# The first 512 columns behind each inner norm in plain float32, in a two-layer transformer encoder

## The chip, the cores and the metric

The kernel runs on one core of a Trainium2 chip. The metric is the time of one execution in microseconds (us), taken on the device; the median of three executions before the change is 2357.82 us (2348.81 to 2362.06).

The names of the engines are those of the profile: PE multiplies matrices (PEld is its loading of weights), DVE is the vector engine, ACT the scalar engine, POOL the third one, SP issues the transfers (DMA) from main memory.

## What is computed

Two layers of an encoder over 256 tokens of width 2048, all in float32. In each layer a modulation vector `mod = silu(c) @ w_mod + b_mod` gives a shift, a scale and a gate for each of two halves. The two halves are the mixers and the FFN:

```python
h = layer_norm(x) * (1.0 + scale_m) + shift_m
proj = h @ w_in[l]
uv, q_c, kv_c, k_r, sb, sc, sh, ag = jnp.split(proj, IN_SPLITS, axis=-1)
...
y = jnp.concatenate([y_a, y_b, y_c, y_d], axis=-1) @ w_out[l]
x = layer_norm(ALPHA * x + (1.0 + gate_m) * y, post_mix_g[l], post_mix_b[l])
h = layer_norm(x) * (1.0 + scale_f) + shift_f
gate, val = jnp.split(h @ w_up, 2, axis=-1)
gate = causal_dwconv(gate, w_conv, b_conv)
y = (jax.nn.silu(gate) * val) @ w_down
x = layer_norm(ALPHA * x + (1.0 + gate_f) * y, post_ffn_g[l], post_ffn_b[l])
```

`y_a` is a gated MLP mixer (its two inputs are called U and V here), `y_b` an attention (B), `y_c` a short convolution (C and E), `y_d` a convolution of 31 taps with a norm over channels (D). The FFN is 5632 wide.

## The kernel before, in words

**Tiles.** The 256 tokens are two token tiles of 128. A product has the contraction of 2048 in 16 tiles of 128 (`kt`). The weights come from memory as `wraw`, 128 x 2048 floats each, on SP's queue. Outputs lie channel-major (128 channels on the partitions, 256 tokens beside one another) for the mixers and the FFN's first product, token-major for `w_out` and `w_down` (out_proj).

**Split products.** Most products are not done in plain float32. A weight tile is split into a rounded part `whi` (ACT, line 403) and the remainder `wlo` (DVE, line 404), an activation in the same way (`hT`, lines 422 and 423), and PE adds three products: `whi` with the high part of `hT`, `whi` with its low part, `wlo` with the high part. There are 4 buffers for `whi` and 4 for `wlo`. For the first items behind a norm a split may go to spare buffers instead (`thi`, `tlo`: the argument `spare`). Layer 0's mixers and a part of its w_out take unsplit float32 products with `wexact` tiles that need no ACT or DVE work; a `wexact` tile sits in a `whi` or `wlo` buffer.

**Groups.** `group` runs a block of columns over all 16 `kt` with moving operands of 256 tokens; `group2` does so with 512 (high and low part beside one another), and adds the two halves afterwards (ACT `second`, line 1200). `run` and `stream` put an item's loads, splits and products in program order, with the products of an item always one item behind its loads (`pending`, `flush`).

**The order on an engine.** Each engine runs its instructions in the order that a scheduler gave them from the program order and their dependences. What is told to wait behind a norm (`hold`: the next 4 splits and 6 modulation steps) is told so by a dependence.

**Inner norms.** There are three between the first product and the last: behind layer 0's w_out (called site 1 here), behind layer 0's w_down (site 2), behind layer 1's w_out (site 3). Out_proj ends with a residual, a LayerNorm `p` with gains, and the statistics of the next norm, `r` (DVE, lines 586 to 616, token tile 0 first, while PE multiplies token tile 1). Then `to_hT` does, for each token tile and each quarter (4 `kt`): `xn` on ACT (normalise), four transposes on PE (`ps_xT`, line 535), scale and shift on ACT (token tile 0) or DVE (token tile 1) into `hf`, and the split of `hf` into `hT`. The order of the eight steps interleaves the token tiles, and the first product takes all 256 tokens of a `kt`.

**Behind the norms.** Site 1 is followed by the FFN of layer 0: group `g0a` (1024 gate columns), interleaved by hand with `v0a` (512 value columns); its last quarter of `hT` is made in between (`LATE_KT`, a part of the modulation comes only then). Site 2 is followed by layer 1's mixers in the order D, U, V, B, C, E; site 3 by layer 1's FFN, beginning with a `group2`.

**Modulation.** The modulation's own weights pass through SP's queue in steps called mods here, each a DMA and a DVE step (line 211, 2.35 us for 128 x 2048), placed by a rate for each stage (`RATES`), at one or two of an item's loads. What a norm needs and what isn't there yet is done ahead of it at once (`need`, `needs`). PE sums the result over partitions (`ps_mod`). Small steps such as the convolution of D are spread by `bg` (`STEPS`), and what is left of them is drained at the end.

Of the kernel before, what the change touches and what calls it, by code (L numbers as in the profile page):

```python
# [13 lines left out]
P = 128  # L14
D = 2048
S = 256
DEPTH = 2
# [37 lines left out]
def encoder_kernel(ctx: ExitStack, tc: tile.TileContext, A: dict, consts: bass.AP, out: bass.AP):  # L55
# [262 lines left out]
    def phase(l, name):  # L318
        pace["rate"] = RATES[l][name]
# [97 lines left out]
    def new_hT():  # L417
        hT[:] = [act_pair("hT") for _ in range(KT // 2)]

    def split(dst, src):  # L420
        hi, lo = dst[:2]
# [103 lines left out]
    def to_hT(t, k0, nkt, r, l, m_shift, m_scale, hF=None):  # L525

        n = nkt * P
        xn = tmp_tile("xn")[:, :n]
        i = ident_act(xn, X[t][:, k0 * P : k0 * P + n], r[:, 0:1], r[:, 1:2])
        for m in (m_shift, m_scale):  # L530
            for name in {MOD_BY[(l, m, k0 + j)] for j in range(nkt)}:
                tc.add_manual_dep(i.ins, name, data_dep, reason="PSUM is free for the modulation first")
        ps = ms_tile("ps_xT")
        for j in range(nkt):
            pe.transpose(ps[:, j * P : (j + 1) * P], xn[:, j * P : (j + 1) * P], ident)  # L535
        if hF is None:
            h3 = tmp_tile("hf")[:, :n].rearrange("p (j t) -> p j t", j=nkt)
        else:
            h3 = hF[k0 // 4][:, k0 % 4 : k0 % 4 + nkt, t * P : (t + 1) * P]
        for j in range(nkt):  # L540
            src, dst = ps[:, j * P : (j + 1) * P], h3[:, j, :]
            sc, sh = MOD[(l, m_scale, k0 + j)], MOD[(l, m_shift, k0 + j)]
            if t == 0:
                ident_act(dst, src, sc, sh)
            else:
                dve.tensor_scalar(out=dst, in0=src, scalar1=sc, scalar2=sh, op0=ALU.mult, op1=ALU.add)  # L546
        for j in range(0, nkt, 2):
            hl = [h[:, :, t * P : (t + 1) * P] for h in hT[(k0 + j) // 2][:2]]
            split(hl, h3[:, j : j + 2, :])


    CHUNKS = ((0, 1024), (1024, 512), (1536, 512))

# [127 lines left out]
    def mixers(l, w_in, Y, hF=None, between=None):  # L681
# [467 lines left out]
    def ffn_up(l, G):  # L1149
        pf = PF[l]  # L1150
        w = A["ffn_w_up"][l]
        col = lambda k, j: pf[:, k * NF + j : k * NF + j + 1]
        def gated_pairs(cps, _):
            for b in range(4):
                if b % 2 == 0:
                    G.append(slot("g").rearrange("p (j s) -> p j s", j=4))
                src = cps[b].rearrange("p (j s) -> p j s", j=2)
                act.copy(G[b // 2][:, 2 * (b % 2) : 2 * (b % 2) + 2, :], src)
            for j in range(8):
                background.append(lambda j=j: gate_conv(j))  # L1160

        def valued_pairs(cps, _):
            drain_background()
            for b in range(2):
# [3 lines left out]
        def gate_conv(j):  # L1168
# [6 lines left out]
                )  # L1175
            act.activation(out=x, in_=u, func=AF.Silu)

        if l == 0:
# [8 lines left out]
            for g, u in ((gg, 5), (gv, 2), (gg, 6), (gg, 7), (gv, 3)):  # L1187
                stream(lambda: g[1](u), lambda item, g=g, u=u: g[2](item, u))
            pending.extend([gg[3], gv[3]])

        for c0 in range(0, D_FF, 512):
            gi, j0 = c0 // 512, c0 // P
# [90 lines left out]

        return before

    after_norm = []

    def modulated(l, m_shift, m_scale, quarters=4):
        def rest(r):
            needs(l, m_shift, m_scale)()  # L1290
            for q in range(quarters, 4):
                for t in range(2):
                    to_hT(t, 4 * q, 4, r[t], l, m_shift, m_scale)

        def then(r):
            if quarters < 4:
                after_norm.append(lambda: rest(r))
            new_hT()
            for kind, n in (("split", 4), ("mod", 6)):
                hold[kind] = [last_norm[0].ins.name, n]  # L1300
            for t, q in ((0, 0), (0, 1), (1, 0), (0, 2), (1, 1), (0, 3), (1, 2), (1, 3)):
                if q < quarters:
                    to_hT(t, 4 * q, 4, r[t], l, m_shift, m_scale)

        return then

    def gate(l, m):
        def make():
# [5 lines left out]
    for l in range(DEPTH):  # L1314
        Y = {}
        if l == 0:
            hF = [slot(f"hF{q}").rearrange("p (j s) -> p j s", j=4) for q in range(4)]
            mixers(l, A["w_in"][l], Y, hF, lambda q: piece(q, hF))
        else:
            mixers(l, A["w_in"][l], Y)  # L1320
        phase(l, "out")
        flush()
        out_proj(
            l,
            A["w_out"][l],
            [Y[n] for n in "abcd"],
            list(range(KT)),
            gate(l, GATE_M),
            f"o{l}",
            A["post_mix_g"][l],  # L1330
            A["post_mix_b"][l],
            needs(l, SHIFT_F, SCALE_F, k1=LATE_KT if l == 0 else KT),
            modulated(l, SHIFT_F, SCALE_F, LATE_KT // 4 if l == 0 else 4),
            plain=(1024, 1536) if l == 0 else (),
        )
# [7 lines left out]
        out_proj(  # L1343
            l,
            A["ffn_w_down"][l],
            G,
            list(range(NF)),
            gate(l, GATE_F),
            f"d{l}",
            A["post_ffn_g"][l],  # L1350
            A["post_ffn_b"][l],
            needs(l + 1, SHIFT_M, SCALE_M) if l + 1 < DEPTH else None,
            modulated(l + 1, SHIFT_M, SCALE_M) if l + 1 < DEPTH else None,
        )
    flush()

# [62 lines left out]
```

## Time and profile before

| | us |
|---|---|
| median of three executions | 2357.82 (2348.81 to 2362.06) |
| span of the profiled execution | 2350.0 |
| PE busy in it | 2259.1 |
| DVE busy | 1811.3 |
| ACT busy | 1036.4 |
| PE waiting for `xn` ahead of the transposes at L535 (10 waits) | 36.5 |

Only the span is recorded of the profiled execution, not a time of its own; it lies inside the range of the three executions, 7.8 us under their median. In the profile's lines a group is named line, engine, operation, output<-inputs; sizes are partitions x elements. A float32 product shows as two records, a split (fp32r) one as one record. A timeline's row has the start, the time to the end of the run of equal instructions, and in brackets the idle time ahead of it with what ended it.

### The profile page before, as it was taken

How to read it: one execution, taken by the hardware profiler on the slowest of the kernel's cores; microseconds unless marked ns; L12 is line 12 of the kernel's file. 1: busy time of each engine (PE TensorE's matmuls, PEld its weight loads, DVE VectorE, ACT ScalarE, POOL GpSimd, SP SyncE). 2: the span in 40 equal slices, each digit the busy share in tenths (PEclk: the TensorE clock that was granted, in tenths of full speed). 3: DMA queues.
4: the chain of work that ended last, by engine and by line, in shares of the span. 5: the costliest groups of instructions: out<-in, count | busy, mean ns of one | idle time of the engine just before them, and what ended most of it. 6: DMA issues, size and time to landing. Idle time of an engine off the chain costs nothing. (4 is left out here: it accounts for less than half of the span.)

```text
span 2350.0 us, 30996 instructions
## 1 busy us (share of the span) xinstructions
PE 2259.1 (96%) x12183; PEld 1924.6 (82%) x12183; DVE 1811.3 (77%) x2293; ACT 1036.4 (44%) x1478; POOL 38.0 (2%) x59
## 2 busy tenths in 40 slices
PE   6899999799999999999989999989999999999998
PEld 4688886498888888888878999867888888888786
DVE  6868987789888887988976986787676656665676
ACT  2221241345455544544535434435454455554553
POOL 2000000000000000000000000000000000000000
PEclk9899999899999999999998999999999999999999
DMA  9999779498889898898756566856767655556554
GB/s 338 368 316 329 285 274 383 159 341 309 308 312 329 291 327 296 309 328 294 274 186 228 191 227 199 297 185 233 236 234 247 205 190 181 193 183 197 179 197 144
DMA packets 226491, 605.17 MB, mean 258 GB/s; under 512 B 14484, under 2 KB 27012, under 8 KB 208676
## 3 DMA queue, kind: packets, MB, share of 16 engines
q1 hardware_dynamic: 225560, 602.29, 73.2%
q8 instruction: 95, 1.56, 0.3%
q0 software_dynamic: 784, 0.90, 0.1%
q14 instruction: 52, 0.43, 0.0%
HBM read 601.05 MB, written 2.10 MB: 257 GB/s over the span
## 5 line engine op out<-in xcount | busy, mean ns | idle before, releaser
L404 DVE TENSOR_TENSOR wlo<-wraw,whi 128x1024 fp32r<-128x1024 f32 (+1 forms) x645 | 775.7, 1216 | 360.4 <-ACT whi L403 354.5
L403 ACT CAST whi<-wraw 128x1024 fp32r<-128x1024 f32 (+1 forms) x645 | 670.9, 1046 | 817.8 <-PE g_c L83 208.2
L83 PE MATMUL v_c<-hT,whi 128*128 128x512 f32 x1344 | 473.1, 397 | 0.0
L83 PE MATMUL g_c<-hT,whi 128*128 128x512 f32 x1272 | 450.3, 398 | 0.0
L83 PE MATMUL d<-whi,a 128*128 128x512 f32 x1344 | 388.4, 391 | 0.3 <-ACT whi L403 0.3
L211 DVE SCALAR_TENSOR_TENSOR macc<-wmod,cact,macc 128x2048 f32<-128x2048 f32 (+2 forms) x180 | 358.1, 1993 | 38.9 <-DMA wmod<-in_w_mod_dram 38.2
L83 PE MATMUL v_c<-hT,wlo 128*128 128x256 f32 x1344 | 376.9, 281 | 0.0
L83 PE MATMUL g_c<-hT,wlo 128*128 128x256 f32 x1272 | 358.2, 282 | 0.0
L83 PEld LDWEIGHTS v_c<-hT,whi 128*128 128x128 f32 x1344 | 252.3, 188 | 60.1
L83 PEld LDWEIGHTS d<-whi,a 128*128 128x128 f32 x1344 | 252.9, 188 | 53.7 <-ACT whi L403 0.8
L83 PEld LDWEIGHTS g_c<-hT,whi 128*128 128x128 f32 x1272 | 239.7, 188 | 57.4 <-issue 0.5
L83 PEld LDWEIGHTS v_c<-hT,wlo 128*128 128x128 f32 x1344 | 254.0, 189 | 0.3 <-DVE wlo L404 0.2
L83 PEld LDWEIGHTS g_c<-hT,wlo 128*128 128x128 f32 x1272 | 241.4, 190 | 0.7 <-issue 0.5
L83 PE MATMUL d<-wlo,a 128*128 128x512 f32 x672 | 234.4, 391 | 0.8 <-DVE wlo L404 0.8
L83 PEld LDWEIGHTS d<-wlo,a 128*128 128x128 f32 x672 | 126.6, 188 | 27.6 <-DVE wlo L404 1.1
L83 PE MATMUL o<-whi,a 128*128 128x512 f32 x352 | 99.6, 392 | 0.1
L708 DVE SCALAR_TENSOR_TENSOR convD<-gluD,pm,convD 128x245 f32<-128x245 f32 (+23 forms) x240 | 98.7, 467 | 0.5
L423 DVE TENSOR_TENSOR a<-g,a 128x512 fp32r<-128x512 f32 x132 | 89.0, 686 | 0.0
L83 PE MATMUL D_c<-hT,whi 128*128 128x256 f32 x432 | 83.9, 294 | 2.5 <-ACT hT L422 2.0
L422 ACT CAST a<-g 128x512 fp32r<-128x512 f32 x132 | 81.3, 616 | 7.2 <-PE d L83 6.0
L211 DVE SCALAR_TENSOR_TENSOR qacc<-wmod,cact,qacc 128x1024 f32<-128x1024 f32 (+1 forms) x75 | 80.3, 1070 | 2.6 <-DMA wmod<-in_w_mod_dram 0.5
L83 PEld LDWEIGHTS o<-whi,a 128*128 128x128 f32 x352 | 66.0, 188 | 14.4 <-ACT whi L403 0.5
(310 smaller groups left out, 2667.4 us busy)
## 6 DMA issues: line engine op xcount, KB each, us to landing
wraw<-in_ffn_w_up_dram SPq DMA_DIRECT2D x176, 1024.0 KB, 5.4
wmod<-in_w_mod_dram SPq DMA_DIRECT2D x136, 1024.0 KB, 5.7
wraw<-in_ffn_w_down_dram SPq DMA_DIRECT2D x88, 1024.0 KB, 5.2
wraw<-in_w_in_dram SPq DMA_DIRECT2D x34, 1024.0 KB, 5.9
wmod<-in_w_mod_dram SPq DMA_DIRECT2D x64, 512.0 KB, 8.0
wmod<-in_w_mod_dram SPq DMA_DIRECT2D x32, 768.0 KB, 6.8
wraw<-in_w_out_dram SPq DMA_DIRECT2D x24, 1024.0 KB, 7.3
wexact<-in_w_in_dram SPq DMA_DIRECT2D x44, 512.0 KB, 6.5
```

Of the source, the lines that this page charges most:

```text
L83: pe.matmul(o, lhsT, rhs, start=start, stop=stop, skip_group_check=True)
L211: i = dve.scalar_tensor_tensor(out=acc, in0=w, scalar=col, in1=acc, op0=ALU.mult, op1=ALU.add)
L403: act.copy(hi[:, :m], r)
L404: i = dve.tensor_tensor(out=lo[:, :m], in0=r, in1=hi[:, :m].bitcast(F32), op=ALU.subtract)
L422: act.copy(hi, src)
L423: dve.tensor_tensor(out=lo, in0=src, in1=hi.bitcast(F32), op=ALU.subtract)
L708: dve.scalar_tensor_tensor(out=yd[:, j, 30 - k :], in0=glu[:, j, : S - 30 + k], scalar=CW(k, j), in1=yd[:, j, 30 - k :], op0=ALU.mult, op1 ...
```

## The change

Behind each of the three inner norms a new function, `first_group`, computes the first 512 columns. It takes plain float32 products: `wexact` tiles in all eight `whi` and `wlo` buffers (16 `kt` x 512 columns), and moving operands of 128 tokens, token tile 0 through all its quarters first, then token tile 1. The modulated activations stay as float32 in `hF0` to `hF3`; the splits into `hT` come behind these products. The number of held weight splits is 8 instead of 4.

At site 1 the first group is the gate's first half `g00`, with three quarters; the groups behind it are `v00` and `g01`, each 512 wide, and the fourth quarter (with its modulation, norm and 256-token products) is done by `late` between their items. At site 2 the first group is U; D follows it instead of leading, and U has no small steps beside it any more. At site 3 it is the gate's first 512 columns, `g10`. The rate of mods in layer 0's down stage goes from 0.7 to 0.83.

```diff
-    dict(B=1.3, C=1.6, out=2.1, first=1.2, up=0.68, down=0.7),
+    dict(B=1.3, C=1.6, out=2.1, first=1.2, up=0.68, down=0.83),
...
+    def first_group(w, c0, name, l, m_shift, m_scale, quarters=4):
+
+        hF = [slot(f"hF{q}").rearrange("p (j s) -> p j s", j=4) for q in range(4)]
+        items = [weights(w, 0, 4, c0, 512, True)]
+        flush()
+        items += [weights(w, 4 * q, 4, c0, 512, True) for q in range(1, 4)]
+        r = after_norm.pop()
+        hT[:] = [act_pair("hT") for _ in range(KT // 2)]
+        for kind, n in (("split", 8), ("mod", 6)):
+            hold[kind] = [last_norm[0].ins.name, n]
+        cps = [acc_tile(f"{name}_c{i}") for i in range(2)]
...
+        steps = [(t, q) for t in range(2) for q in range(quarters)]
+        turned(*steps[0])
+        for n, (t, q) in enumerate(steps):
+            if n + 1 < len(steps):
+                turned(*steps[n + 1])
+            products(q, t * P, (t + 1) * P, (t, q) == (0, 0), q == 3)
+        for q in range(quarters):
+            splits(q)
+
+        def rest():
+            for q in range(quarters, 4):
+                for t in range(2):
+                    turned(t, q)
+                products(q, 0, S, False, q == 3)
+                splits(q)
+
+        return cps, rest
...
-        gd = group(w_in, C_AG, 1024, f"D{l}", mix_d, spare=1)
-        gu = group(w_in, C_UV, 512, f"U{l}", mix_u, nk=4, bg=STEPS[1]["U"])
+        phase(l, "U")
+        mix_u(first_group(w_in, C_UV, f"U{l}", l, SHIFT_M, SCALE_M)[0], None)
         phase(l, "D")
-        run(gd)
-        phase(l, "U")
-        run(gu)
+        run(group(w_in, C_AG, 1024, f"D{l}", mix_d, spare=1))
...
+        cps, rest = first_group(w, 0, f"g{l}0", l, SHIFT_F, SCALE_F, LATE_KT // 4 if l == 0 else 4)
         if l == 0:
 
-            gg = group(w, 0, 1024, "g0a", gated_pairs, spare=1)
-            gv = group(w, D_FF, 512, "v0a", valued_pairs, nk=4)
+            gv = group(w, D_FF, 512, "v00", valued_pairs, nk=4, spare=1)
+            gg = group(w, 512, 512, "g01", lambda cps, _: gated_first(cps, 4), nk=4)
             phase(l, "first")
-            for g, u in ((gg, 0), (gg, 1), (gv, 0), (gg, 2), (gg, 3), (gv, 1), (gg, 4)):
+
+            def late():
+                needs(l, SHIFT_F, SCALE_F)()
+                rest()
+                gated_first(cps)
+
+            for g, u in ((gv, 0), (gg, 0), (gv, 1), (gg, 1), (gv, 2), (gg, 2)):
                 stream(lambda: g[1](u), lambda item, g=g, u=u: g[2](item, u))
-            pending.append(after_norm.pop())
+            pending.append(late)
...
-            if l > 0 or gi > 1:
-                run(group2(w, c0, f"g{l}{gi}", gated, spare=int(gi == 0)))
+            if gi > int(l == 0):
+                run(group2(w, c0, f"g{l}{gi}", gated))
```

In the rows below, the number behind a name is a buffer's; a name in `ps_` is in PSUM, and `[waits ...]` names the engines or transfers whose semaphores the instruction waits for.

**PE at site 1, the late quarter.** Before, on PE, the sums of the late modulation stand among the products of `g0a`, each piece by itself:

```order
L83 MATMUL g0a_c3_2797<-hT_2678,whi_3118 128x256 x2
L83 MATMUL ps_mod_3238<-ones_84,macc_1846 128x1 [waits DVE_49]
L83 MATMUL g0a_c0_2794<-hT_2678,wlo_3119 128x256 [waits DVE_49]
...
L83 MATMUL ps_mod_3246<-ones_84,macc_2248 128x1 [waits DVE_49]
L83 MATMUL g0a_c0_2794<-hT_2679,whi_3182 128x256 [waits Activation_49]
...
L535 MATMUL ps_xT_3256<-cst_82,xn_3254 128x128 [waits PE_49,Activation_49]
L83 MATMUL g0a_c1_2795<-hT_2679,whi_3182 128x256
```

After it, on PE, the same steps for `g00` stand in one row, with no product of another group between the sums and the fourth quarter's products:

```order
L83 MATMUL g01_c1_2961<-hT_2689,wlo_3157 128x256
L83 MATMUL ps_mod_3272<-bcol0_97,cst_82 128x4
L83 MATMUL ps_mod_3272<-ones_84,macc_1846 128x1 [waits DVE_49]
L83 MATMUL ps_mod_3286<-bcol0_97,cst_82 128x4
L83 MATMUL ps_mod_3286<-ones_84,macc_2248 128x1 [waits DVE_49]
L533 MATMUL ps_xT_3296<-cst_82,xn_3294 128x128 [waits PE_49,Activation_49]
L533 MATMUL ps_xT_3307<-cst_82,xn_3305 128x128 [waits PE_49,Activation_49]
L83 MATMUL g00_c0_2692<-hF3_2547,wexact_2680 128x256 [waits DMAHW4_49,DVE_49,Activation_49]
L83 MATMUL g00_c1_2693<-hF3_2547,wexact_2680 128x256 x2
```

What moved: the products that stood between the sums, the transposes and the late quarter are now ahead of or behind the whole row.

**PE at site 2.** Before, on PE, behind the last product of `d` (layer 0's w_down) stand the sums of the last modulation, four quarters' transposes, and D:

```order
L83 MATMUL d0_153610_8934<-whi_9237,a_9244 128x512
L83 MATMUL ps_mod_9379<-ones_84,macc_8068 128x1 [waits DVE_49]
L535 MATMUL ps_xT_9465<-cst_82,xn_9463 128x128 [waits PE_49,Activation_49]
L535 MATMUL ps_xT_9481<-cst_82,xn_9479 128x128 [waits PE_49,Activation_49]
L535 MATMUL ps_xT_9497<-cst_82,xn_9495 128x128 [waits Activation_49]
L535 MATMUL ps_xT_9513<-cst_82,xn_9511 128x128 [waits Activation_49]
L83 MATMUL D1_c0_9605<-hT_9455,thi_9249 128x256 [waits Activation_49]
```

After it, on PE, two quarters stand ahead of the first product, and no sum of the modulation:

```order
L83 MATMUL d0_153610_8816<-whi_9119,a_9126 128x512
L533 MATMUL ps_xT_9353<-cst_82,xn_9351 128x128 [waits PE_49,Activation_49]
L533 MATMUL ps_xT_9364<-cst_82,xn_9362 128x128 [waits PE_49,Activation_49]
L83 MATMUL U1_c0_9349<-hF0_9129,wexact_9133 128x128 [waits DMAHW2_49,Activation_49]
L83 MATMUL U1_c1_9350<-hF0_9129,wexact_9133 128x128 x2
```

The sums of the modulation are further up in `d` after the change, and the transposes of the other quarters stand between U's products.

**ACT at the step from U to D.** Before, ACT casts D's first weights (`thi`) ahead of the norm, and U's `ya` (GELU) follows U with other work of ACT around it. After, on ACT, `thi_9588`, which D's first product takes, stands behind U's two `ya`:

```order
L403 CAST whi_9602<-wraw_9596 128x1024 [waits DMAHW5_49,PE_49]
L403 CAST whi_9660<-wraw_9658 128x1024 [waits DMAHW7_49,DMAHW1_49,PE_49]
L810 ACT_TABLE_LOAD
L810 ACTIVATE ya_9583<-U1_c0_9349 128x512 [waits PE_49]
L810 ACTIVATE ya_9583<-U1_c1_9350 128x512 [waits PE_49]
L403 CAST thi_9588<-wraw_9586 128x1024
```

On PE, after, the last products of U are followed at once by that `thi_9588`:

```order
L83 MATMUL U1_c0_9349<-hF3_9132,wexact_9337 128x128 [waits DVE_49]
L83 MATMUL U1_c1_9350<-hF3_9132,wexact_9337 128x128 x2
L83 MATMUL U1_c0_9349<-hF3_9132,wexact_9339 128x128 [waits DVE_49]
L83 MATMUL U1_c1_9350<-hF3_9132,wexact_9339 128x128 x2
L83 MATMUL D1_c0_9606<-hT_9341,thi_9588 128x256 [waits Activation_49]
```

The cast that D's first product takes has moved from ahead of the norm to behind U's end. `whi_9660` lies in the buffer that `wexact_9337` had.

**PE in layer 1's E.** The norm over channels of D (`ps_mean`, `ps_var`, `ps_rD`, with ACT, DVE and POOL steps between them) is the last of the small steps. After, on PE:

```order
L83 MATMUL ps_mean_11661<-convD_10075,ones_84 128x256 x2
L83 MATMUL E1_c0_11470<-hT_9347,whi_11598 128x256 [waits Activation_49]
L83 MATMUL E1_c0_11470<-hT_9347,wlo_11599 128x256 [waits DVE_49]
...
L83 MATMUL ps_var_11674<-ones_84,sqD0_11670 128x1 [waits PE_49,Activation_49]
...
L83 MATMUL E1_c0_11470<-hT_9348,whi_11602 128x256 x2
L83 MATMUL ps_rD_11689<-dgD_11686,ones_84 128x256 [waits DVE_49]
```

Before, `ps_mean`, `ps_var` and `ps_rD` stood at E's beginning; now the second half of `ps_mean` stands behind three quarters of E (`hT_9341` to `hT_9346` of eight), and the whole chain must end in the last quarter.

More of the change, by code (lines that the diff above doesn't have):

```diff
@@ L415, in encoder_kernel @@
     hT = []
-    def new_hT():
-        hT[:] = [act_pair("hT") for _ in range(KT // 2)]
+    after_norm = []
     def split(dst, src):
@@ L546, in to_hT @@
                 dve.tensor_scalar(out=dst, in0=src, scalar1=sc, scalar2=sh, op0=ALU.mult, op1=ALU.add)
+        if hF is not None:
+            return
         for j in range(0, nkt, 2):
@@ L549, in to_hT, with turned, products, splits @@
             split(hl, h3[:, j : j + 2, :])
+    def first_group(w, c0, name, l, m_shift, m_scale, quarters=4):
[8 more added lines that the diff above has]
+        cps = [acc_tile(f"{name}_c{i}") for i in range(2)]
+        def turned(t, q):
+            to_hT(t, 4 * q, 4, r[t], l, m_shift, m_scale, hF)
+        def products(q, lo, hi, first, last):
+            for k in range(4):
+                for i in range(4):
+                    mm(
+                        cps[i // 2][:, (i % 2) * S + lo : (i % 2) * S + hi],
+                        items[q][k][0][:, i * P : (i + 1) * P],
+                        hF[q][:, k, lo:hi],
+                        first and k == 0 and i % 2 == 0,
+                        last and k == 3,
+                    )
+        def splits(q):
+            for k in range(0, 4, 2):
+                split(hT[2 * q + k // 2], hF[q][:, k : k + 2, :])
+        steps = [(t, q) for t in range(2) for q in range(quarters)]
[13 more added lines that the diff above has]
+        return cps, rest
     CHUNKS = ((0, 1024), (1024, 512), (1536, 512))
@@ L1152, in ffn_up @@
         col = lambda k, j: pf[:, k * NF + j : k * NF + j + 1]
[L1153 to L1160, printed above, removed]
         def valued_pairs(cps, _):
@@ L1284, in needs, with normed @@
         return before
[L1286 to L1305, printed above, removed]
+    def normed(r):
+        after_norm[:] = [r]
     def gate(l, m):
@@ L1332, in encoder_kernel @@
             needs(l, SHIFT_F, SCALE_F, k1=LATE_KT if l == 0 else KT),
-            modulated(l, SHIFT_F, SCALE_F, LATE_KT // 4 if l == 0 else 4),
+            normed,
             plain=(1024, 1536) if l == 0 else (),
@@ L1352, in encoder_kernel @@
             needs(l + 1, SHIFT_M, SCALE_M) if l + 1 < DEPTH else None,
-            modulated(l + 1, SHIFT_M, SCALE_M) if l + 1 < DEPTH else None,
+            normed if l + 1 < DEPTH else None,
         )
```

14 lines of the change are left out of this document (11 added, 3 removed).

## The prediction

> **What bounds the kernel now.** I begin with the page's busy times and its chain of work that ended last.
>
> ```profile
> span 2350.0 us, 30996 instructions
> PE 2259.1 (96%) x12183; PEld 1924.6 (82%) x12183; DVE 1811.3 (77%) x2293; ACT 1036.4 (44%) x1478; POOL 38.0 (2%) x59
> PE g_c L83 11%; PE v_c L83 11%; PE d L83 10%; DVE x L610 0%; DVE x L607 0%; DVE st_o1q L616 0%; PE ps_gate L83 0%; DVE wlo L404 0%; PE ps_xT L535 0%; DVE yg L586 0%; DVE x L587 0%; DVE hT L423 0%; DVE hf L546 0%; POOL rs_o1r L106 0%; DVE st_d L590 0%
> ```
>
> PE is busy for 96% of the span and the chain consists of its products, with short pieces of the norms on DVE. So time goes up by what PE has to do in addition, and down only by what PE idles less: 2350.0 - 2259.1 = 90.9 us in all. The list of waits, read for PE, says where the idle time is.
>
> ```profile
> PE ps_xT L535 <- ACT xn L86: 36.5, 10, 7.8
> ```
>
> That is the largest entry: 36.5 us in ten waits of the transposes behind the inner norms. PE's timeline at the three sites shows the whole hole, from the last product to the first full product.
>
> ```profile
> 435.85 3.60 PE L83 MATMUL o<-wexact,yd 128*128 128x512 f32 x8
> 444.87 1.12 PE L535 MATMUL ps_xT<-cst,xn 128*128 128x128 f32 x4 [5.42 <-ACT xn L86]
> 457.38 1.22 PE L83 MATMUL g0a_c<-hT,thi 128*128 128x256 f32 x4 [0.79 <-ACT hT L422]
> ...
> 1218.60 0.39 PE L83 MATMUL d<-whi,a 128*128 128x512 f32 x1
> 1221.70 6.58 PE L83 MATMUL ps_mod<-ones,macc 128*128 128x1 f32 x32 [2.71 <-DVE macc L211]
> 1240.90 1.20 PE L83 MATMUL D_c<-hT,thi 128*128 128x256 f32 x4
> ...
> 1573.08 0.39 PE L83 MATMUL o<-whi,a 128*128 128x512 f32 x1
> 1581.24 1.12 PE L535 MATMUL ps_xT<-cst,xn 128*128 128x128 f32 x4 [7.77 <-ACT xn L86]
> 1594.11 0.79 PE L83 MATMUL g_c<-hT,thi 128*128 128x512 f32 x1 [1.40 <-DVE hT L423]
> ```
>
> The holes are 457.38 - 439.45 = 17.9 us, 1240.90 - 1218.99 = 21.9 us and 1594.11 - 1573.47 = 20.6 us. After the first transposes, 9 to 13 us pass until both token tiles are there. The change starts on token tile 0 alone, so it can have most of that; it pays with dearer products.
>
> **Part 1: the earlier start.** DVE's timeline shows what stands within the norm of token tile 0 and, by the order of the changed program, no longer does: splits at all three sites, and two mods at site 2.
>
> ```profile
> 431.25 1.21 DVE L404 TENSOR_TENSOR tlo<-wraw,thi 128x1024 fp32r<-128x1024 f32 x1
> 432.37 1.22 DVE L404 TENSOR_TENSOR wlo<-wraw,whi 128x1024 fp32r<-128x1024 f32 x1
> ...
> 1211.40 2.35 DVE L211 SCALAR_TENSOR_TENSOR macc<-wmod,cact,macc 128x2048 f32<-128x2048 f32 x1
> 1216.24 1.22 DVE L404 TENSOR_TENSOR wlo<-wraw,whi 128x1024 fp32r<-128x1024 f32 x1
> 1219.30 2.35 DVE L211 SCALAR_TENSOR_TENSOR macc<-wmod,cact,macc 128x2048 f32<-128x2048 f32 x1
> 1226.28 0.16 DVE L517 SCALAR_TENSOR_TENSOR rs_d0r<-mv_d0r,rs_d0r 128x1 f32<-128x1 f32 x1
> ...
> 1570.56 1.22 DVE L404 TENSOR_TENSOR wlo<-wraw,whi 128x1024 fp32r<-128x1024 f32 x1
> ```
>
> Their starts are 1.1 to 2.3 us apart, so the norm is ready 2.3 us earlier at site 1, about 5.9 us at site 2 (2.35 + 1.22 + 2.35) and 1.2 us at site 3. From there to the first plain product stand two `xn`, four transposes and one slice of scale and shift, in ACT's rows:
>
> ```profile
> 1228.63 0.81 ACT L86 ACTIVATE xn<-x,rs_d0r 128x512 f32<-128x512 f32 x1
> ...
> 1231.23 1.50 ACT L86 ACTIVATE hf<-ps_xT,mod,mod 128x128 f32<-128x128 f32 x4
> ```
>
> - Site 1: transposes at 444.87 - 2.3 = 442.6, 1.1 for them, 0.4 for a slice (a quarter of 1.50): products at 444.2, **13.2 us** earlier.
> - Site 2: the norm is ready at 1226.4 - 5.9 = 1220.5; 0.8 and 0.8 for two `xn`, transposes within that and behind it, a slice: products at 1222.9, **18.0 us** earlier. But the 32 records of `ps_mod` now stand among the products of `d`; at full clock some 3.4 us (half of 6.58, which ran slow), so **-3.4**.
> - Site 3: transposes at 1580.0, products at 1581.6, **12.5 us** earlier.
>
> Token tile 1 is no new wait: by the rows above both tiles were there 12.5 to 12.9 us behind the first transposes at sites 1 and 3, and tile 0's products (part 2) take 10.8 to 14.4 us, 1.7 more with the slow start.
>
> **Part 2: the dearer products.** Which row has a float32 product on 128 columns? Layer 0's gated MLP, and for 256 columns layer 0's U; each product is two records.
>
> ```profile
> 208.04 1.60 PE L83 MATMUL ps_mix<-wT,va 128*128 128x128 f32 x12
> 209.49 1.89 PE L83 MATMUL B_c<-hF,wexact 128*128 128x256 f32 x8
> ...
> 38.60 3.62 PE L83 MATMUL U<-hF,wexact 128*128 128x256 f32 x16
> 42.05 1.89 PE L83 MATMUL D_c<-hF,wexact 128*128 128x256 f32 x8
> ...
> 461.34 0.40 PE L83 MATMUL g0a_c<-hT,whi 128*128 128x256 f32 x2
> 461.70 0.40 PE L83 MATMUL g0a_c<-hT,whi 128*128 128x256 f32 x2
> ...
> 1598.14 0.39 PE L83 MATMUL g_c<-hT,whi 128*128 128x512 f32 x1
> 1598.48 0.39 PE L83 MATMUL g_c<-hT,whi 128*128 128x512 f32 x1
> ```
>
> Six products of 128 columns take 209.49 - 208.04 = 1.45 us, 0.242 each; eight of 256 take 3.45 us, 0.431 each, thus 0.216 for half. I take **0.225**, nearer the longer run. The split way costs 461.70 - 461.34 = 0.36 us for a `kt` and 128 channels (three products), and 0.34 in a `group2`; 512 columns are 64 of these, 23.0 and 21.8 us. The plain way takes 64 x 2 x 0.225 = 28.8 us. So **-5.8** at site 2, **-7.0** at site 3; at site 1, three quarters take 96 x 0.225 = 21.6 against 17.3, **-4.3**, and the last quarter 16 x 0.431 = 6.9 against 5.8, **-1.2**. The bounds of 0.216 and 0.242 move the total of 352 such products by +3.2 and -6.0 us. Besides, two groups of transposes at each site leave the hole and stand among products: 2 x 0.35, **-0.7** each. The start at the slow clock costs plain products about 0.5 more than it cost the split ones: **-0.5** each.
>
> How dear is a restart? Two equal runs show it, one behind products, one behind a hole of 1.91 us:
>
> ```profile
> 43.78 3.60 PE L83 MATMUL V<-wexact,hF 128*128 128x512 f32 x8
> ...
> 67.14 5.37 PE L83 MATMUL V<-wexact,hF 128*128 128x512 f32 x8 [1.91 <-DMA wexact<-in_w_in_dram]
> ```
>
> 5.37 - 3.60 = 1.8 us lost. I take 1.7 for a hole of 2 us or more, nothing for shorter ones.
>
> [...]
>
> **Part 3: the new hand-overs.** Three places, all by the order shown ahead.
>
> *Site 1, `late`.* The sums, two `xn`, the transposes and the slices come one behind the other, and PE has nothing else in its queue. 0.27 for the modulation's copy (estimated like the `mod` steps around it), 2 x 0.81, 0.35 for transposes, 0.35 for a slice of DVE, and four hand-overs of 0.1: 3.0 us, and 1.7 for the clock: **-4.7**. What that wait keeps back on PE is everything behind it, thus `v00`. Besides, `macc_2248` may be late, and until then the fourth quarter holds one of four pairs of `whi`/`wlo` buffers: 0 to 5 us, I take **-1.5**.
>
> *Site 2, U to D.* D's first product waits for `thi_9588`. Ahead of it on ACT stand `whi_9660`, a table load and two `ya`:
>
> ```profile
> 1313.09 1.28 ACT L762 ACT_TABLE_LOAD   x1
> 1314.38 1.24 ACT L762 ACTIVATE ya<-U_c 128x512 f32<-128x512 f32 x2
> 1315.52 1.04 ACT L403 CAST whi<-wraw 128x1024 fp32r<-128x1024 f32 x1
> ```
>
> `whi_9660` waits for the buffer of `wexact_9337`, free 8 products (1.8 us) ahead of U's end; then 1.05 and 1.28 end 0.5 us behind U, two `ya` 1.2 us later, `thi_9588` another 1.05: a hole of **2.85** us and 1.7 of clock. Before, that work had cover from `D`, whose first weights were cast ahead of the norm.
>
> *Site 3.* `v10` takes its first split from the buffer of the first quarter, early enough, but the splits of `hT` stand on the same engines: **-1.0** (0 to -2).
>
> *E in layer 1.* U's small steps go, so the channel norm of D ends at E's end, with 1.5 and 1.2 us of products between its sums. DVE's rows for two of the steps:
>
> ```profile
> 1463.44 0.16 DVE L742 TENSOR_SCALAR rd<-ps_var 128x2 f32<-128x2 f32 x1 [1.39 <-PE ps_var L83]
> 1465.34 0.48 DVE L748 TENSOR_SCALAR dgD<-cst,rd 128x128 f32<-128x128 f32 x2 [0.59 <-POOL rd L106]
> ```
>
> From `ps_var` to the end of `dgD` pass 1465.82 - 1463.44 = 2.4 us, against 1.2 of cover; for the steps from `ps_mean` to `ps_var` I take 0.8 in the same way. **-2.0** (0 to -4).
>
> **Part 4: more mods in layer 0's down stage.** By the order of SP the stage has 27 in place of 23, of which 2 stood in the norm.
>
> ```profile
> 480.00:500.00 20.00, 20.00 (x167) 19.81 (x166) 18.13 (x22) 7.59 (x9) 0.00 (x0) 1.00 1.03 393
> 960.00:990.00 30.00, 30.00 (x149) 25.34 (x148) 29.77 (x32) 17.52 (x25) 0.00 (x0) 1.00 0.94 346
> 1020.00:1050.00 30.00, 30.00 (x134) 24.86 (x133) 25.36 (x21) 15.64 (x18) 0.00 (x0) 1.00 0.91 320
> ```
>
> (Columns: sum, PE, PEld, DVE, ACT, POOL, clock, DMA share, GB/s.) The DMA engines are at 0.91 to 0.94 there. A load and its mods grow from 1.70 to 1.83 units, 7.6%, which makes 0.98 to 1.01. The highest flow I see is 393 GB/s, so most of it may pass: **-2.0** (0 to -9). DVE, 25.4 of 30 us, gets about 2 us more and is no bound.
>
> **The sum.**
> - Site 1: 13.2 - 4.3 - 1.2 - 0.7 - 0.5 - 4.7 - 1.5 = +0.3
> - Site 2: 18.0 - 3.4 - 5.8 - 0.7 - 0.5 - 4.55 = +3.05
> - Site 3: 12.5 - 7.0 - 0.7 - 0.5 - 1.0 = +3.3
> - E and down: -4.0
>
> That is 2.65 us saved: the span goes from 2350.0 to 2347.3, and on the scale of the median, 7.8 us above it, 2357.8 to **2355.2**. A gain of 44 us at three starts is nearly paid back.
>
> **The rivals.**
> 1. *The hand-overs are covered.* PE's queue has products behind the hole only, which speaks against it; but `macc` and the casts may come earlier than I set them, and ACT, at 44%, has room. Without the 4.7 and 1.5 of `late` and the 4.55 of U to D: 2355.2 - 10.8 = **2344.4**.
> 2. *Slower: DMA becomes the bound in layer 0's down stage.* If the share reaches 1.00 from 960 to 1080, six more MB cost 6 / 0.35 = 17 us of transfer, against 7% of 120 = 8 us of room; up to 9 us of waits for weights, I take 8 in place of 2: **2361.2**. It decides from 7% more load on; for it speaks 0.94, against it 393 GB/s.
> 3. *Holes of about 3 us leave the clock up.* 2 x 1.7 less: **2351.8**. The row of V speaks against it.
> 4. *The first `wexact` weights come late.* They can be issued only when the last products release their buffers (about 1215 at site 2); 4 MB at 0.35 MB per us take 12 us, and the first quarter is there at about 1219 to 1221. Four us late at sites 2 and 3: **2363**.
> 5. *A 128-column product costs as much as one of 256*, that is 0.431: 352 x 0.206 = 73 us, **2428**. The row of `ps_mix`, 0.242, speaks against it.
>
> **How the numbers follow.** Chances: forecast 0.42 (own range 2347 to 2363 from the bounds of its terms), rival 1 0.24, rival 2 0.14, rival 3 0.08, rival 4 0.08, rival 5 0.04. The predicted time is the forecast's. The range for 8 in 10 takes in rivals 1 to 4 without their outer ends: **2340 to 2367**. A measurement of this kernel can tell about 0.5%, 11.8 us, from no change: faster is below 2346.0, slower above 2369.6. Faster: 0.18 of rival 1, 0.06 of the forecast's lower tail, 0.02 of rival 3, **0.26**. Slower: 0.04 of rival 5, 0.03 of rival 2, 0.02 of rival 4, **0.09**. The rest, **0.65**, is same.
>
> **What the profile after would show.** First products near 444, 1223 and 1582, with 128-column float32 products at 0.225 spacing. A hole of about 3 us at `g00`'s fourth quarter and one of about 2.9 us ahead of D, each followed by slow products; short waits at `ps_var` and `ps_rD`. The prediction is wrong upwards if those holes are missing, downwards if the shares of DMA near 1000 reach 1.00 with PE waiting for `whi`, or if `U1` waits for `wexact`.

## The result and the profile after

The changed kernel takes 2342.81 us (median of 5, 2333.62 to 2345.61), against 2357.82 us before (median of 5, 2348.81 to 2363.85): a ratio of 0.9929, with a 95% interval of 0.9906 to 0.9951. Two later series of 6 executions gave 0.9940 (0.9916 to 0.9964) and 0.9944 (0.9924 to 0.9965). So it is faster by some 0.6 to 0.7%, 13 to 17 us, and none of the three intervals reaches 1; 2.6 us were forecast. The profiled execution has a span of 2341.0 us, 9.0 less than the one before.

The page of the changed kernel, its busy times and its chain:

```profile
span 2341.0 us, 31348 instructions
PE 2273.2 (97%) x12407; PEld 1940.7 (83%) x12407; DVE 1784.2 (76%) x2241; ACT 1012.0 (43%) x1429; POOL 36.0 (2%) x59
PE g_c L83 11%; PE v_c L83 11%; PE d L83 9%; DMA wraw<-in_ffn_w_down_dram 0%; DVE x L658 0%; PE ps_xT L533 0%; DVE x L655 0%; PE ps_gate L83 0%; DVE wlo L404 0%; DVE st_o1q L664 0%; ACT whi L403 0%; DVE yg L634 0%; DVE tlo L404 0%; DVE x L635 0%; ACT thi L403 0%
```

PE is busy 14 us longer, and its idle time went from 90.9 to 67.8 us. The list of waits for PE (us in total, times, longest) shows what is left of the 36.5 us in ten waits before, a new wait ahead of D, and one for the modulation at site 1:

```profile
PE ps_xT L533 <- ACT xn L86: 11.3, 4, 6.0
...
PE D_c L83 <- ACT thi L403: 2.7, 1, 2.7
...
PE ps_mod L83 <- DVE macc L211: 1.5, 1, 1.5
```

PE's timeline of the changed kernel at the three sites, from the last product ahead of the norm:

```profile
435.22 3.60 PE L83 MATMUL o<-wexact,yd 128*128 128x512 f32 x8
441.21 1.93 PE L533 MATMUL ps_xT<-cst,xn 128*128 128x128 f32 x8 [2.39 <-ACT xn L86]
442.93 4.62 PE L83 MATMUL g_c<-hF,wexact 128*128 128x128 f32 x32
...
1223.78 0.39 PE L83 MATMUL d<-whi,a 128*128 128x512 f32 x1
1225.92 1.36 PE L533 MATMUL ps_xT<-cst,xn 128*128 128x128 f32 x8 [1.75 <-ACT xn L86]
1227.12 3.84 PE L83 MATMUL U_c<-hF,wexact 128*128 128x128 f32 x32
1230.80 0.60 PE L533 MATMUL ps_xT<-cst,xn 128*128 128x128 f32 x4
1231.23 3.74 PE L83 MATMUL U_c<-hF,wexact 128*128 128x128 f32 x32
1234.81 0.60 PE L533 MATMUL ps_xT<-cst,xn 128*128 128x128 f32 x4
...
1251.29 7.31 PE L83 MATMUL U_c<-hF,wexact 128*128 128x128 f32 x64
1261.27 1.21 PE L83 MATMUL D_c<-hT,thi 128*128 128x256 f32 x8 [2.68 <-ACT thi L403]
...
1569.29 0.39 PE L83 MATMUL o<-whi,a 128*128 128x512 f32 x1
1575.66 1.97 PE L533 MATMUL ps_xT<-cst,xn 128*128 128x128 f32 x8 [5.99 <-ACT xn L86]
```

The holes from the last product to the first one are now 442.93 - 438.82 = 4.1 us and 1227.12 - 1224.17 = 2.95 us (17.9 and 21.9 before); at site 3 the first product, at 1577.43, comes 7.75 us behind (20.6). Sixteen products of 128 columns take 1234.81 - 1231.23 = 3.58 us, 0.224 each.

Where did the time go? The first products of each stage cut the span into stretches; with the 334 to 335 us ahead of layer 0's w_out they add up to it. `v01` and `v10` are the value columns' second group of layer 0 and first group of layer 1. The table has both profiles, and a second profile of each kernel (below):

| stretch, us | before | again | after | again |
|---|---|---|---|---|
| w_out of layer 0 to v01 (site 1) | 199.4 | 199.7 | 195.6 | 201.5 |
| v01 to down of layer 0 | 437.9 | 442.0 | 444.0 | 441.1 |
| down to V of layer 1 (site 2) | 342.7 | 339.8 | 334.0 | 337.2 |
| V to w_out of layer 1 | 167.1 | 168.3 | 168.6 | 169.4 |
| w_out to v10 (site 3) | 138.3 | 139.0 | 134.2 | 134.1 |
| v10 to the end | 729.8 | 729.7 | 730.5 | 721.6 |

Site 2, with what belongs to it, gained 3 to 9 us and site 3 some 4 to 5; site 1 between 4 gained and 2 lost. The other rows hold the same or nearly the same work, yet vary by up to 9 us; what is known of that comes at the end.

### The profile page after: what moved, and what is told of

It reads as the page before. It is cut to its first block, busy times and chain, and to the rows that moved or that the text cites. A ratio compares the mean times of both kernels' runs of the same rounds, so it can differ in the third digit from the quotient of the medians.

```text
span 2341.0 us, 31348 instructions
## 1 busy us (share of the span) xinstructions
PE 2273.2 (97%) x12407; PEld 1940.7 (83%) x12407; DVE 1784.2 (76%) x2241; ACT 1012.0 (43%) x1429; POOL 36.0 (2%) x59
## 5 line engine op out<-in xcount | busy, mean ns | idle before, releaser
L404 DVE TENSOR_TENSOR wlo<-wraw,whi 128x1024 fp32r<-128x1024 f32 (+1 forms) x622 | 748.0, 1215 | 352.2 <-ACT whi L403 344.6
L403 ACT CAST whi<-wraw 128x1024 fp32r<-128x1024 f32 (+1 forms) x622 | 645.8, 1045 | 759.9 <-PE g_c L83 224.3
L83 PE MATMUL v_c<-hT,whi 128*128 128x512 f32 (+1 forms) x1456 | 499.3, 391 | 0.0
L83 PE MATMUL g_c<-hT,whi 128*128 128x512 f32 (+1 forms) x1344 | 452.4, 387 | 0.0
L83 PE MATMUL v_c<-hT,wlo 128*128 128x256 f32 x1400 | 395.2, 282 | 0.0
L83 PEld LDWEIGHTS v_c<-hT,whi 128*128 128x128 f32 x1456 | 271.6, 189 | 62.8 <-ACT whi L403 0.2
L83 PEld LDWEIGHTS g_c<-hT,whi 128*128 128x128 f32 x1344 | 248.3, 188 | 56.0
L83 PEld LDWEIGHTS v_c<-hT,wlo 128*128 128x128 f32 x1400 | 266.3, 190 | 0.4 <-DVE wlo L404 0.2
L756 DVE SCALAR_TENSOR_TENSOR convD<-gluD,pm,convD 128x255 f32<-128x255 f32 (+26 forms) x240 | 98.8, 459 | 0.5
L1210 DVE SCALAR_TENSOR_TENSOR u<-g,pf,u 128x254 f32<-128x254 f32 (+1 forms) x176 | 74.3, 477 | 10.7 <-ACT u L86 10.7
```

The costliest lines, as they stand in the source:

```text
L83: pe.matmul(o, lhsT, rhs, start=start, stop=stop, skip_group_check=True)
L403: act.copy(hi[:, :m], r)
L404: i = dve.tensor_tensor(out=lo[:, :m], in0=r, in1=hi[:, :m].bitcast(F32), op=ALU.subtract)
L756: dve.scalar_tensor_tensor(out=yd[:, j, 30 - k :], in0=glu[:, j, : S - 30 + k], scalar=CW(k, j), in1=yd[:, j, 30 - k :], op0=ALU.mult, op1 ...
L1210: dve.scalar_tensor_tensor(out=u[:, sh:], in0=x[:, : S - sh], scalar=col(k, j), in1=u[:, sh:], op0=ALU.mult, op1=ALU.add)
```

## The experiments

**The token order, the rate, and the hand-over.** Four kernels, each with one part of the change undone, alone or mended. The first takes both token tiles at once, still in plain float32:

```diff
-        steps = [(t, q) for t in range(2) for q in range(quarters)]
...
-            products(q, t * P, (t + 1) * P, (t, q) == (0, 0), q == 3)
+        for t, q in ((0, 0), (0, 1), (1, 0)):
+            turned(t, q)
+        for q in range(quarters):
...
+            products(q, 0, S, q == 0, q == 3)
```

> Changed kernel, but the first products take both token tiles at once (256 columns, plain float32 as before this edit), so PE must wait for token tile 1's norm again. Theory (the gain is the start on token tile 0, and the clock that the short holes keep up): each of the three holes grows by 7 to 9 us and its restart loses 1.7 to 3.4 us of clock, 25 to 37 us in all, ratio to the kernel before 1.003 to 1.009. Rival (the gain is that splits and modulation steps have left the norm's way on DVE): under 5 us are lost, ratio at most 0.995.

Measured: 2367.48 us (10 executions), ratio 1.0043 (1.0020 to 1.0065), thus 0.4% slower than the kernel before. Its span is 2359.5 us, 18.5 over the changed kernel's. PE's timeline of this kernel at site 2:

```profile
1234.37 1.80 PE L533 MATMUL ps_xT<-cst,xn 128*128 128x128 f32 x8 [1.74 <-ACT xn L86]
1246.31 1.97 PE L533 MATMUL ps_xT<-cst,xn 128*128 128x128 f32 x8 [10.14 <-ACT xn L86]
1249.86 7.79 PE L83 MATMUL U_c<-hF,wexact 128*128 128x256 f32 x30
```

The second transposes, token tile 1's, wait 10.14 us. The three stretches with the sites grow by 11.0, 13.1 and 6.6 us against the changed kernel's first profile. The rival falls: plain float32 without the token order costs more than it brings, even with the new rate, and without the start on token tile 0 nothing of the gain is left.

The rate alone, undone in the changed kernel and put into the kernel before:

```diff
-    dict(B=1.3, C=1.6, out=2.1, first=1.2, up=0.68, down=0.83),
+    dict(B=1.3, C=1.6, out=2.1, first=1.2, up=0.68, down=0.7),
```

> Changed kernel with the old rate 0.7 in layer 0's down stage, so four steps of the modulation are again done at once at site 2, three of them within the norm. Theory: 3 x 2.35 = 7 us more in the norm, and the sums of the modulation back in the hole (6.6 us at half clock instead of 3.4 elsewhere), less 0 to 2 us of relief in the down stage: the hole at site 2 grows from 3 us to 11 to 16 us, 8 to 12 us slower than the changed kernel. Rival (the higher rate crowds the DMA queues in the down stage as much as it frees the norm): within 3 us of the changed kernel.

Measured: 2348.03 us (10), ratio 0.9959 (0.9939 to 0.9979). This kernel and the kernel before have the same rate, so the rest of the change, the early start with its dearer products, pays by itself, some 0.4%. Against the changed kernel (0.9929 to 0.9944) it is 0.2 to 0.3% slower, with intervals that overlap. PE's timeline of this kernel at site 2:

```profile
1216.82 0.39 PE L83 MATMUL d<-whi,a 128*128 128x512 f32 x1
1222.73 6.99 PE L83 MATMUL ps_mod<-ones,macc 128*128 128x1 f32 x32 [5.52 <-DVE macc L211]
1230.93 1.97 PE L533 MATMUL ps_xT<-cst,xn 128*128 128x128 f32 x8 [1.21 <-ACT xn L86]
1232.69 3.52 PE L83 MATMUL U_c<-hF,wexact 128*128 128x128 f32 x19
```

The hole is 1232.69 - 1217.21 = 15.5 us instead of 2.95, as the theory had it. The stretch from down to V is 343.9 us, 9.9 over the changed kernel's first profile and 6.7 over its second; the theory's 8 to 12 holds against the first alone, and the times show less.

> Kernel before with only the new rate of 0.83. Theory: 4.7 us of steps leave the norm at site 2, and the sums of the modulation (3.4 us at full clock) go among the products of the down stage; the two cancel within 2 us, since products still wait for both token tiles: ratio 0.998 to 1.002. Rival (the gain comes from the rate): 8 us or more faster, ratio below 0.997.

Measured: 2344.84 us (7), ratio 0.9947 (0.9924 to 0.9970). By the times that is the rival's result, 0.5% from the rate alone. The stretches give it only a part: from down to V this kernel takes 338.3 us against 342.7 and 339.8, so 1.5 to 4.4 us; its last stretch has 720.7 us against 729.8 and 729.7, where the rate has no part. The theory's "cancel within 2 us" was too low as well, and a step of it did not happen: the sums of the modulation did not go among the products of the down stage. In PE's timeline of this kernel they still stand behind its last product:

```profile
1226.41 0.39 PE L83 MATMUL d<-whi,a 128*128 128x512 f32 x1
1226.64 4.20 PE L83 MATMUL ps_mod<-ones,macc 128*128 128x1 f32 x32
```

The hole from the last product to D's first one is 1243.82 - 1226.80 = 17.0 us, against 21.9 and 21.0 in the two profiles before, so 4 to 5 us less. How much of the 0.5% is the rate's stays open. With it stays open what the early start adds at the new rate: by the times 0.9947 and 0.9929 to 0.9944 don't part. The three stretches with the sites, added up, take 680.4 and 678.5 us before, 674.5 with the rate alone, 674.0 with the early start alone, and 663.8, 672.8 and 667.4 with both (the third is from a later run of the changed kernel). That fits some 5 us for each part, but the three sums of one kernel differ by 9 us.

The hand-over from U to D, mended:

```diff
-        mix_u(first_group(w_in, C_UV, f"U{l}", l, SHIFT_M, SCALE_M)[0], None)
+        sums_u = first_group(w_in, C_UV, f"U{l}", l, SHIFT_M, SCALE_M)[0]
+        pending.append(lambda: mix_u(sums_u, None))
```

> Changed kernel with U's two GELU steps put behind the first casts of D, so D's first product no longer waits for a cast behind U's end. Theory: the hole of 2.7 us ahead of D goes, and nothing more, since the clock was kept across it: about 2.5 us faster than the changed kernel, ratio 0.992. Rival (the wait goes on to the next casts, which want the buffers of U's last quarter): same hole a few products later, no gain.

Measured: 2335.40 us (4), ratio 0.9911 (0.9876 to 0.9945). PE's timeline of this kernel:

```profile
1250.32 7.31 PE L83 MATMUL U_c<-hF,wexact 128*128 128x128 f32 x64
1257.39 0.48 PE L83 MATMUL D_c<-hT,thi 128*128 128x256 f32 x2
```

The hole is gone and did not come back behind it; down to V takes 329.2 us, 4.8 less than in the changed kernel's first profile. Of these, 3.2 lie behind U's first product (77.4 us to V against 80.6); the others lie in the down stage, which the edit does not touch. The interval overlaps that of the changed kernel, so the gain is shown by the profile, not by the times.

**The late quarter, one item earlier.** The changed kernel's profile also has holes of 1.5, 1.2 and 0.6 us at site 1, in PE's timeline:

```profile
504.49 1.05 PE L83 MATMUL ps_mod<-ones,macc 128*128 128x1 f32 x8 [1.53 <-DVE macc L211]
506.74 1.97 PE L533 MATMUL ps_xT<-cst,xn 128*128 128x128 f32 x8 [1.20 <-ACT xn L86]
509.33 8.94 PE L83 MATMUL g_c<-hF,wexact 128*128 128x256 f32 x32 [0.62 <-ACT hF L86]
```

The edit puts the sums, `xn` and transposes of that quarter ahead of the last products of `g01`, which lets the scheduler spread them:

```diff
+            def early():
+                needs(l, SHIFT_F, SCALE_F)()
+                rest_turned()
...
             for g, u in ((gv, 0), (gg, 0), (gv, 1), (gg, 1), (gv, 2), (gg, 2)):
+                if (g, u) == (gg, 2):
+                    pending.append(early)
```

> Changed kernel with the sums, the norm's quarter and the transposes of the late quarter put into the program one item earlier, ahead of the last products of g01. Theory: PE gets products between those steps, the holes of 1.5, 1.2 and 0.6 us at site 1 shrink to under 1.5 in all, the two slow windows of the clock that follow them (6.8 us at half speed, 3.4 us lost) go: 3 to 5.5 us faster than the changed kernel. Rival (what is late is the modulation on DVE, whatever the order on PE): the waits stay, no gain.

Measured: 2331.64 us (6), ratio 0.9908 (0.9887 to 0.9930). PE's timeline at the place, and the windows of PE there (span, busy, granted clock, DMA share, GB/s), of the changed kernel and then of this one:

```profile
507.44 0.95 PE L83 MATMUL ps_mod<-ones,macc 128*128 128x1 f32 x8
509.59 1.36 PE L533 MATMUL ps_xT<-cst,xn 128*128 128x128 f32 x8
511.57 7.14 PE L83 MATMUL g_c<-hF,wexact 128*128 128x256 f32 x32 [0.62 <-ACT hF L86]
```

```profile
504.40:517.90 13.50, 11.59 (x48) 0.75 0.82 297
```

```profile
504.40:518.40 14.00, 13.30 (x86) 1.00 0.93 337
```

Two holes are gone, and the clock stays at 1.00 where it was 0.75. The stretch of site 1 takes 194.2 us, 1.4 and 7.3 less than in the changed kernel's two profiles; in the latter the sum had waited 2.7 us for `macc`. The scheduler's order changed at site 2 too: the sums of the last modulation stand behind `d`'s last product again, so the hole there is 6.4 us instead of 2.95, and the down stage is 3.5 us shorter.

**Both mends.**

> Changed kernel with U's GELU steps behind D's first casts and the late quarter's steps one item earlier. Theory: the gains add, 5.5 to 8 us faster than the changed kernel, ratio to the kernel before 0.989 to 0.991. Rival (one hides the other, or the late quarter's gain does not come): 2.5 us, ratio 0.992.

Measured: 2337.92 us (6), ratio 0.9936 (0.9911 to 0.9961), which speaks for the rival; yet the span of its profile, 2325.4 us, is 5.5 under that of the kernel with one mend. That profile is of the fastest of its six executions, so the spans alone don't settle it. So both were run again beside the changed kernel on one chip.

> Both mends again, on one chip with the two kernels that it is compared with. Theory (the U to D mend adds 2.7 us of hole, and what clock it lost, to the gain of the late quarter, and its higher median of 2337.9 us came from the spread of executions): median 2 to 5 us under late_r2, ratio 0.988 to 0.991. Rival (the two mends hinder one another): median over that of late_r2 again.

> The late quarter one item earlier, again. Theory: 4 to 8 us faster than after_r2, ratio 0.989 to 0.992. Rival (its first median was a lucky draw): within 2 us of after_r2.

> The changed kernel a third time, as the base of the two others. Theory: median 2336 to 2345, ratio 0.992 to 0.995, and in its profile a hole of 2.7 us ahead of D as before, with or without a slow window of the clock behind it.

Measured: 2334.58 us for both mends (0.9912, 0.9887 to 0.9936), 2335.56 us for the late quarter alone (0.9919, 0.9890 to 0.9947), 2341.46 us for the changed kernel (0.9944, 0.9924 to 0.9965). The late quarter's mend is worth some 6 us by the medians of both series, though the intervals overlap; that both beat one by more than 1 us isn't settled by the times. In the stretches they do: 190.4 and 329.6 us for sites 1 and 2, against 190.0 and 333.9 with the late quarter alone, and 195.3 and 337.2 of the changed kernel in the same series. So the hand-over's mend brings another 4 us at site 2. By the stretches both mends are the best version run; the times don't part them from the single ones, and the lowest median of all is the first one of the late quarter alone.

**Each kernel once more.** The last stretch takes 730 us in some profiles and 721 in others, and by the time for a group of 512 columns in it (called the rhythm) a slow and a fast kind can be told apart.

> The kernel before once more, with a profile. PE's group2 rows took 22.2 us in some stretches of the profiles and 22.6 us in others, with the same instructions. Theory (the rhythm is drawn anew in each execution and does not belong to the change): this profile shows another mixture of 22.2 and 22.6 than the first one of this kernel, in which nearly all groups of layer 1 took 22.6. Rival (it belongs to the kernel, by its addresses or its order): layer 1 takes 22.6 again throughout.

> The changed kernel once more, with a profile and more executions, for the interval. Theory of a rhythm drawn in each execution: another mixture of 22.2 and 22.6 us than in its first profile, in which layer 1 took 22.6; the median stays within 2334 to 2346. Rival (a property of the kernel): layer 1 takes 22.6 throughout again.

The windows from 1700 to 1900 us of the changed kernel's first and second profile:

```profile
1700.00:1900.00 200.00, 200.00 (x1135) 1.00 0.67 231
```

```profile
1700.00:1900.00 200.00, 200.00 (x1156) 1.00 0.69 237
```

The same program, at a granted clock of 1.00 and without idle time, does 1135 products in one execution and 1156 in the other. So the rhythm does not belong to the kernel alone. The kernel before showed the slow one twice (x1134 and x1133), which leaves open whether it favours it; with the new rate alone, which is set in layer 0, its last stretch was a fast one (720.7 us). Its second span of 2353.2 us and median of 2357.43 us (8 executions; ratio 1.0012, 0.9986 to 1.0037) are like the first.

## Why the prediction was right in its direction and too low in its size

The measured time lies inside the stated range, and the gain has the sign of the forecast. But it is five to six times the forecast's, 2342.81 us is below the forecast's own bounds of 2347 to 2363, and it is under the 2346.0 from which the prediction speaks of faster, to which it gave 0.26. It lies 1.6 us from rival 1's time; that is a coincidence, since what rival 1 needs did not happen.

**Right: the price of plain products and the early start.** Taken as 0.225 us per 128 columns, measured 0.224, so rival 5 falls. The first products came 4.1, 2.95 and 7.75 us behind the last ones (forecast 4.75, 3.9 and 8.1), at once behind the transposes at all three sites, so the first `wexact` weights were there and rival 4 falls.

**Right: the places of the hand-overs.** `late` was to idle for 3.0 us besides the wait for `macc`, and idled 1.2 + 0.6, plus 1.5 for `macc` (forecast 1.5); U to D 2.85, measured 2.68, at the place and by the instruction named. Rival 1, that they are covered, did not happen in the changed kernel, but the mends made it happen, and then its 2344.4 us was undercut.

**Right only in the number: E.** The stretch from V to w_out lost 1.5 us (forecast 2.0), but not by the waits that were forecast. PE did not wait at `ps_var`, and ahead of `ps_rD` as long as before; what is new are two waits for `wlo`. These are PE's waits from 1305 to 1485 us, the first line of the kernel before, the others of the changed one:

```profile
PE ps_rD L83 <- DVE dgD L748: 0.3, 1, 0.3
PE B_c L83 <- DVE wlo L404: 1.1, 1, 1.1
PE E_c L83 <- DVE wlo L404: 0.6, 1, 0.6
PE ps_rD L83 <- DVE dgD L796: 0.3, 1, 0.3
```

So the 2.0 us for the chain in E did not come, and that 1.7 us were lost in other waits is luck.

**Wrong: site 2, mis-sized.** The forecast was +3.05 there and a part of -2.0 for the down stage, thus +1.05; the stretch gained 8.7 us, in the second profiles 2.6. Of the first pair's 7.6 us that were missed, the rows tell this:
- The start was charged with 0.5 more than before, on the assumption that both the old and the new one run at the slow clock. In this pair only the old one did: the windows of PE show D's first 5.2 us at half clock before, and U's first quarter at full clock after (these two in that order):

```profile
1240.90:1246.10 5.20, 4.78 (x23) 0.50 0.70 218
```

```profile
1227.12:1230.80 3.68, 3.68 (x35) 1.00 1.04 392
```

Half of 5.2 us, 2.6, was lost there before and nothing after, so this term was +2.6 instead of -0.5 and is the largest miss, 3.1 us. In the second and third profile of the changed kernel one piece of 3.41 us at half clock lies in U's start. D itself took 1291.8 - 1240.9 = 50.9 us before, 1307.7 - 1261.3 = 46.4 after: these 4.5 us are the same 2.6 and some 1.7 for four groups of four transposes (0.43 each), which now stand in U and which the sum had taken into account.
- The clock behind the hole ahead of D was charged with 1.7 and stayed up in this execution, so nothing was lost. Rival 3 (holes of about 3 us leave the clock up) had that; but in the second profile the same hole of 2.68 us was followed by a slow piece, 0.67 in the mean over 5.2 us:

```profile
1266.76:1272.00 5.24, 5.20 (x28) 0.67 0.57 188
```

So neither the 1.7 nor the 0 holds each time: five of six profiles with that hole had a slow piece behind it, one had none (1.00 from 1256.4 to 1275), and in the kernel with both token tiles at once products slowed behind a hole of 1.62 us at this place too (two with `thi` took 0.52 us, 0.41 in the changed kernel). Nor does the length of the hole alone decide in these rows: 1.8 us were lost behind 1.91 us in the row of V, nothing behind the 2.68 us here. In the clock's record of the first profile of each kernel the slow pieces, all at 0.50, last 3.41 us or a whole multiple of it, up to 23.9 us (but for the last, which the end cuts off).
- The down stage was charged with 2.0. Its DMA share rose at most from 0.92 to 0.96 in the windows up to 1050 us (these two, before and after, columns as in the prediction) and was 0.97 at most in a later one, with no wait of PE for weights:

```profile
990.00:1020.00 30.00, 30.00 (x134) 24.84 (x133) 24.90 (x23) 13.44 (x17) 0.00 (x0) 1.00 0.92 321
990.00:1020.00 30.00, 30.00 (x134) 24.82 (x134) 29.32 (x26) 14.63 (x17) 0.00 (x0) 1.00 0.96 348
```

From its first product to its last the stage took 250.5 against 246.9 us, 3.6 more, which is about what the moved sums cost (3.4 in the sum). So the 2.0 did not come, and rival 2 falls.
- The hole itself shrank by 19.0 us (forecast 18.0).

**Wrong: site 1, too low.** Forecast +0.3, measured +3.8 in the first pair. The hole gave 13.8 us (forecast 13.2), and what follows it cost 10.0 us (forecast 12.9). Two terms of the latter were mis-sized: the idle time of `late` was 1.8 us and not 3.0, and the start at the slow clock, charged with 0.5 more than before, cost 0.9 less, as the windows of PE behind the hole show (before, then after):

```profile
457.38:460.90 3.52, 3.52 (x16) 0.50 0.16 26
442.93:447.39 4.46, 4.46 (x33) 0.80 0.02 6
```

Against that, the clock was down for 6.8 us at `late`'s holes (0.50 from 506.15 to 512.98), up to 3.4 us lost where 1.7 were charged; the rest was not told apart.

The third profile of the changed kernel (195.3) gained about as much; the second one lost 1.8 us. There `macc` came 2.7 us late, the clock was down for 10.2 us behind it instead of 6.8, and 3.4 us had been lost ahead of the norm, in w_out, at half clock behind 24 products with one moving column.

**Right: site 3.** It gained 4.1 us, forecast 3.3.

**The remaining distance.** 9.0 us between the first spans, but 15.0 between the medians. The stretches with unchanged work differ by up to 9 us from one execution to the next, so single profiles can't hold the medians to better than that, nor part the gain into sites to better than that. That the changed kernel drew the faster rhythm more often than the one before would fit (two of its three profiles, none of the two before), but so few profiles don't show it.

## What to carry to other kernels

When a matmul engine waits for two halves of its input in turn, starting on the first half can pay even with products that cost a quarter more (here 128 x 0.224 = 28.7 us for 512 columns against 23.0, and a gain of some 0.4% at an equal rate of the side work), and the start should be costed with the clock: behind holes of 18 to 22 us the first 3.5 to 5 us ran at half clock in the first profile of the kernel before. Test a side setting that was changed along with it by itself: here it brought nearly as much by the times as the whole change, and the two were not told apart. Behind such a start look at the instructions that the next stage's first product waits for, since here a cast standing behind an activation made a hole of its own, and a serial chain (sums, normalise, transpose) wants products from elsewhere ahead of it in program order (here holes of 1.5 and 1.2 us went by that). Compare stretches of work, not only spans, where executions of one program differ by more than the edit.

## What the runs showed of the hardware that was not expected

With the same instructions, a granted clock of 1.00 and no idle time, the split products of the FFN ran at 22.2 us a group of 512 columns in some stretches and at 22.6 in others; over the last stretch of the program that makes 721 or 730 us. What sets it was not found. And 32 products with one moving column keep PE busy by the profile, yet the clock behind them fell to a half for 3.41 us without any idle time, in PE's timeline and window of the changed kernel:

```profile
805.83 3.71 PE L83 MATMUL ps_mod<-ones,macc 128*128 128x1 f32 x32
```

```profile
809.80:813.40 3.60, 3.60 (x14) 0.53 0.00 0
```

The same happened in its second profile behind 24 such products, for twice as long (timeline, then window):

```profile
416.15 3.08 PE L83 MATMUL ps_mod<-ones,macc 128*128 128x1 f32 x24
418.37:425.20 6.83, 6.83 (x12) 0.50 1.04 386
```

In its first profile these 24 products were not followed by a slow piece (1.00 from 418.37 to 425.20), so this too depends on the execution.
